# Up projection: the order of the products with the high and the low weights inside a part of the weight stream

## The chip, the core and the metric

The kernel runs on one core of one Trainium2 chip. The metric is the time of one execution on the device in microseconds (us), taken as the median over several runs. All times of engines come from one profiled execution of the program.

## What is computed

One decoder layer over 256 tokens of width 2048: a mixer (a recurrent group and an attention group side by side), then a gated feed-forward block, then a norm. The part that matters here is the feed-forward block, whose first matrix product is the up projection:

```python
xn = rms_norm(h, g_ffn[l])
u_ff, v_ff = jnp.split(xn @ w_up[l], 2, axis=-1)
u_ff = causal_dwconv(u_ff, ffn_conv_w[l], ffn_conv_b[l])
h = h + (jax.nn.gelu(u_ff) * v_ff) @ w_down[l]
return rms_norm(h, g_final)
```

Here `w_up` is 2048 x 12288 and `w_down` is 6144 x 2048, in float32.

## The kernel before, in words

**Two parts of every number.** Both factors of a product are float32. Each is cut into a high and a low part, so that the cheap float32r products lose little: high x high + high x low + low x high. The activations are kept as tiles `act` of [128 channels, 4 contraction tiles, 2 parts, 256 tokens]. The weights are split when they arrive: ACT writes the high part (`hi`, line 282) and DVE the low part (`lo`, line 283).

**The weight stream.** All weights pass through one list, `parts`. `group` (line 249) makes the parts of a block of columns. For the up projection a group is 256 columns by 16 contraction tiles; it is loaded in two DMAs of 1 MB on the SP queue (line 272, buffer `raw`, 3 of them) and worked through in four parts of 4 contraction tiles each. `run_stream` (line 287) walks the list: it issues loads 5 parts ahead, splits 2 parts ahead, and then calls the product function of the part once for each of its contraction tiles. There are 4 buffers for `hi` and 4 for `lo`; a split writes a buffer only once the products of the part four places earlier have released it. After the last part of a group its `post` function takes the sums out of PSUM.

**The up projection.** `mm_weights_still` (line 325) keeps the weights stationary: 128 x 128 weights are loaded into TensorE, and the activations stream past. For one contraction tile and one of the two halves m of the 256 columns it issues two products into PSUM bank m. The *high product* (line 336) has the high weights stationary and streams both parts of the activations, 512 columns, into the whole bank. The *low product* (line 339) has the low weights stationary and streams the high part of the activations, 256 columns, into the bank's second half. So one contraction tile gives high, low, high, low, and each product brings a weight load of its own (PEld in the profile). In the last contraction tile of a group the order is low, high, low, high, since the high product closes the bank. `halves` adds the two halves of each bank at the end, `post_up_u` and `post_up_v` do the convolution, the activation and the gating.

**Around it.** The feed-forward width is worked through in three pieces. A piece is 16 groups of the up projection (64 parts, 1024 products), then 4 groups of the down projection. The down projection (`moving`, lines 365 to 367) has the activations stationary and streams weights, always 512 columns. The input projection (`mm_weights_still_plain`, lines 320 to 322) has the weights stationary and streams always 256 columns. Nothing but the program's order and the waits for `hi`, `lo` and PSUM sets when a product runs. The framework may place instructions of an engine differently from the order in which they were written.

Of the kernel before, what the change touches and what calls it, by code (L numbers as in the profile page):

```python
# [15 lines left out]
P = 128  # L16
S = 256            # tokens
NB = S // P        # token blocks
D = 2048
KT = D // P        # contraction tiles of the model width  # L20
# [5 lines left out]
NC = 15            # compressed blocks  # L26
CB = 32            # tokens of a compressed block
CS = 16            # its stride
# [4 lines left out]
LOAD = 2048        # elements per partition of one weight load  # L33
PART = 1024        # elements per partition that are split and multiplied at once
LOOK_LOAD = 5      # parts by which loads run ahead
LOOK_SPLIT = 2     # parts by which the splitting runs ahead
FF_CUT = 3         # the feed-forward width is worked through in so many pieces
PACE = 655         # pace of the side work: units per contraction tile of 256 columns that it is put between
TAIL = 8           # contraction tiles at the end that finish the first token block before the second
# [5 lines left out]
class Part:  # L45
    """A piece of the weight stream: its load, and what is done with it once it is on chip."""

    def __init__(self, load, k0, nk, cols, mm, post):
        self.load, self.k0, self.nk, self.cols = load, k0, nk, cols
        self.mm, self.post, self.pre = mm, post, None  # L50
        self.hi = self.lo = None


class Lane:
    """A queue of side tasks (generators that yield the distance to their next step, in units of PACE)."""
# [22 lines left out]
def hymba_block(ctx, tc, x, g_mix, w_in, lru_conv_w, lru_conv_b, lru_wa, lru_ba, lru_wx, lru_bx, lru_lambda,  # L78
# [23 lines left out]
    # ---------------------------------------------------------------- constants and per-channel vectors  # L102
    ident = cst.tile([P, P], F32, name="ident")
    make_identity(nc, ident)
    xr = resp.tile([P, NB, D], F32, name="xr")           # the residual stream, tokens on partitions
# [8 lines left out]
    # keeps the tensor engine warm until the first operands are there  # L114
# [33 lines left out]
    # a compressed block counts for token t once it has ended: 16 n + 31 <= t  # L148
# [23 lines left out]
    # ---------------------------------------------------------------- helpers  # L172
    def inv_sqrt(v, y):
        """y = 1/sqrt(v) for [P, w]: the reciprocal's root, and a Newton step."""
        w = v.shape[-1]
        r = sm.tile([P, w], F32, name="rms_r")
        t = sm.tile([P, w], F32, name="rms_t")
        nc.vector.reciprocal(r, v)
        tc.keep_in_program_order(act(r, r, AF.Sqrt))
        if w == 1:  # L180
            stt(t, r, v, r, op0=OP.mult, op1=OP.mult)
        else:
            tt(t, r, r, op=OP.mult)
            tt(t, t, v, op=OP.mult)
        ts(t, t, -0.5, 1.5, op0=OP.mult, op1=OP.add)
        tt(y, r, t, op=OP.mult)

    def inv_rms(total, n, name):
        """1/sqrt(total/n + eps) for [P, w] sums of squares."""
# [6 lines left out]
    def across(rs, name):  # L196
        """[P, NB] per-token values to [P, S], the same on every partition."""
# [10 lines left out]
    # A float32's 24 bits in two parts of 12, which the float32r products carry without loss: [channel, tile, part, token]  # L208
# [6 lines left out]
    def two_parts(dst, src, gain=None):  # L215
        """dst [P, part, ..] = the two parts of src * gain"""
# [8 lines left out]
    def transpose_in(cg, g, dst):  # L225
        """Columns cg*512.. of the residual stream, times the gain, to [channel, token] in two parts."""
# [10 lines left out]
    junk = cst.tile([P, 512], mybir.dt.bfloat16, name="junk")   # only the sums are used  # L237

    def squares(dst, cg):
        """Sums of squares per token of columns cg*512.. of the residual stream."""  # L240
# [4 lines left out]
    # ---------------------------------------------------------------- the weight stream  # L245
# [3 lines left out]
    def group(w, c0, ncols, kts, mm_fn, post, cuts=None, row0=0):  # L249
        """Weight rows of `kts` contraction tiles by ncols columns; mm_fn(part, j, k, state, kts) per tile. One load  # L250
        is of LOAD elements, or of as many contraction tiles as `cuts` says."""
# [4 lines left out]
        for i, n in enumerate(cuts):  # L256
# [3 lines left out]
            for j in range(0, n, part_k):  # L260
                m = min(part_k, n - j)
                mine.append(Part(ld, k + j, m, ncols, (mm_fn, state, kts), post if k + j + m == kts else None))
        parts.extend(mine)
# [47 lines left out]
    def mm_weights_still_plain(src):  # L311
        """Weights stationary: [column, token], two tiles of 128 columns."""
# [12 lines left out]
    def mm_weights_still(src):  # L325
        """Weights stationary: [column, token], two tiles of 128 columns. A bank takes the products with the high
        parts in its first half, the rest in its second."""
        def fn(p, j, k, st, kts):
            if k == 0:
                st["ps"] = ps_mm.tile([P, 2, 512], F32, name="mm")  # L330
            a = src(k)
            last = k == kts - 1
            for m in range(2):
                o = st["ps"][:, m]
                wh, wl = p.hi[:, j, m * P:(m + 1) * P], p.lo[:, j, m * P:(m + 1) * P]
                both = lambda: mm(o, lhsT=wh, rhs=a.rearrange("p a s -> p (a s)"), start=k == 0, stop=last)  # L336
                if not last:
                    both()
                mm(o[:, S:], lhsT=wl, rhs=a[:, 0], start=False, stop=False)  # L339
                if last:  # L340
                    both()
        return fn

    def halves(dst, ps):
        """dst = the sum of the two halves of a bank"""
# [4 lines left out]
    def normed(a, rs):  # L350
        """a [P, pair, token] *= the tokens' 1/rms"""
        nc.gpsimd.tensor_tensor(a, a, over_pair(shared[rs]), op=OP.mult)  # L352

    def mm_weights_move(src):
        """Weights moving: [token, column], two blocks of 128 tokens."""
# [13 lines left out]
    # ---------------------------------------------------------------- the normalised input  # L369
# [34 lines left out]
    # ---------------------------------------------------------------- input projection and compressor  # L404
    kcat = mix.tile([P, KVH, 2, S], F32, name="kcat")      # keys [d, kv, branch, token]
    vnat = [mix.tile([P, NB, 2, 256], F32R, name=f"vnat{i}") for i in range(2)]   # values [token, block, branch, (kv d)]
# [14 lines left out]
    def blocks(which):  # L421
        """The overlapping blocks: token 16 n + l of block n, plus its position, in two parts."""
# [12 lines left out]
    def mm_cmp(which):  # L435
        """Stationary: both parts of the tokens l and l + 1 of every block; moving: the weights of l and l + 1. The
        products of unlike l go to rows and columns that nothing reads."""
# [52 lines left out]
    def post_values(br):  # L490
        def post(st):
# [5 lines left out]
            if br == 1:  # L497
                # sigmoid(z) = (1 + tanh(z / 2)) / 2
# [14 lines left out]
    # ---------------------------------------------------------------- attention  # L513
    # With 4 blocks of 64 tokens and 16 selected ones, the selection holds every block: its attention is the causal
    # one over all the tokens, whatever the scores of the blocks. With 256 tokens and a window of 512, so is the
    # window's, over its own keys and values.
# [4 lines left out]
    def open_mixers():  # L521
        late["at"] = mixctx.enter_context(tc.tile_pool(name="at", bufs=1))
        late["lr"] = mixctx.enter_context(tc.tile_pool(name="lr", bufs=1))
        # softplus(-lambda) = max(-lambda, 0) + log1p(exp(-|lambda|)), log1p(y) = 2 atanh(y / (2 + y))
# [22 lines left out]
    def attention(g, b):  # L547
# [3 lines left out]
        nk = b + 1                       # key blocks up to the diagonal one  # L551
# [4 lines left out]
        # compressed branch  # L556
# [13 lines left out]
        # selected and window branches  # L570
        w = nk * P
        hpb = 2 // nk                    # heads of a bank
# [22 lines left out]
        # probabilities with keys on partitions, then the products with the values of the three branches  # L595
# [42 lines left out]
    def channel_rms(sq, name):  # L638
        """1/rms per token from squares [channel of 128, token] that are summed over the tiles of channels."""
# [7 lines left out]
    # ---------------------------------------------------------------- RG-LRU  # L647
    lru_sq = cst.tile([P, S], F32, name="lru_sq")
    halfway = []                         # two of [channel, tile, (1 - a | gated input), token], for 4 tiles each
# [10 lines left out]
    def lru(i, xp):  # L660
# [24 lines left out]
        for m in range(2):  # L685
# [7 lines left out]
            # sigmoid(z) = (1 + tanh(z / 2)) / 2  # L693
            act(r[:, m], gp[:, :S], AF.Tanh, scale=0.5, bias=late["vh"][:, t:t + 1])
            act(iu[:, m], gp[:, S:], AF.Tanh, scale=0.5, bias=late["vh"][:, 8 + t:9 + t])
            # a = exp(-z); 1 - a = (1 + a) tanh(z / 2), without the cancellation
# [16 lines left out]
    def recurrence():  # L713
        room = scratch_new()
        ms = [room[:, :, h] for h in range(2)]
        for m, w in zip(ms, halfway):
            stt(m, w[:, :, 0], 2.0, w[:, :, 0], op0=OP.subtract, op1=OP.mult)                          # a^2 - 1
            nc.gpsimd.tensor_scalar(w[:, :, 0], w[:, :, 0], -1.0, 1.0, op0=OP.mult, op1=OP.add)        # a
# [30 lines left out]
    # ---------------------------------------------------------------- output projection  # L749
# [25 lines left out]
    # ---------------------------------------------------------------- feed-forward  # L775
    FT = FF // P // FF_CUT               # tiles of one piece
# [50 lines left out]
    def mm_tail(p, j, k, st, kts):  # L827
        """As mm_weights_move for the last columns, but the first token block comes to its end first."""
# [36 lines left out]
    # ---------------------------------------------------------------- the order of the stream  # L865
    wi, wo, wu, wd = w_in[0], w_out[0], w_up[0], w_down[0]
    def by_turns(a, b):
        """The parts of two groups, of which each is one load: by turns, two loads to a buffer."""
# [7 lines left out]
    # two groups at once as the columns of x come in, the first of them in smaller pieces  # L876
# [66 lines left out]
```

## Time and profile before

| | us |
|---|---|
| median of 3 runs | 1186.98 |
| lowest and highest run | 1184.58, 1187.15 |
| span of the profiled execution | 1185.0 |
| TensorE busy in it | 1169.7 |
| VectorE busy | 766.8 |
| ScalarE busy | 593.1 |

The span runs from the first to the last instruction of the program. The profile gives no separate total for that execution; its span is 1.98 us below the median of the runs. A start in the timeline is the moment at which the engine begins an instruction. Since TensorE overlaps the end of one product with the beginning of the next, the durations of neighbouring products overlap, and the cost of a product is the step from its start to the next start. The chain of waits shows the same as pieces that don't overlap.

### The profile page before, as it was taken

How to read it: one execution, taken by the hardware profiler on the slowest of the kernel's cores; microseconds unless marked ns; L12 is line 12 of the kernel's file. 1: busy time of each engine (PE TensorE's matmuls, PEld its weight loads, DVE VectorE, ACT ScalarE, POOL GpSimd, SP SyncE). 2: the span in 40 equal slices, each digit the busy share in tenths (PEclk: the TensorE clock that was granted, in tenths of full speed). 3: DMA queues.
4: the chain of work that ended last, by engine and by line, in shares of the span. 5: the costliest groups of instructions: out<-in, count | busy, mean ns of one | idle time of the engine just before them, and what ended most of it. 6: DMA issues, size and time to landing. Idle time of an engine off the chain costs nothing.

```text
span 1185.0 us, 16730 instructions
## 1 busy us (share of the span) xinstructions
PE 1169.7 (99%) x6727; PEld 1021.5 (86%) x6727; DVE 766.8 (65%) x981; ACT 593.1 (50%) x803; POOL 159.5 (13%) x181
## 2 busy tenths in 40 slices
PE   8999999999999999999999999999999999999997
PEld 8999999898788888888888888888888888888885
DVE  4775778779766766666454766666454666666554
ACT  5554546786446554444333444444333454445444
POOL 3210224113200110110000110110000110110000
PEclk8999999999999999999999999999999999999999
DMA  9676544354655555565556555565555565565562
GB/s 295 178 221 213 160 134 157 121 165 136 217 192 177 176 180 192 176 200 179 204 186 196 179 194 180 178 208 182 187 204 185 176 207 180 178 193 183 194 202 81
DMA packets 182397, 217.60 MB, mean 184 GB/s; under 512 B 4064, under 2 KB 147584, under 8 KB 182192
## 3 DMA queue, kind: packets, MB, share of 16 engines
q1 hardware_dynamic: 180928, 213.07, 55.2%
q0 software_dynamic: 1072, 2.41, 0.6%
q8 instruction: 52, 0.85, 0.3%
q10 hardware_dynamic: 320, 1.06, 0.2%
q14 instruction: 25, 0.20, 0.0%
HBM read 214.43 MB, written 2.10 MB: 183 GB/s over the span
## 4 chain that ended last, share of the span: by engine, by line
PE 91%; DVE 2%; ACT 0%; issue 0%; POOL 0%; DVEq 0%
PE mm L336 30%; PE mm L339 15%; PE mm L366 9%; PE mm L367 9%; PE mm L365 9%; PE mm L322 4%; PE mm L320 4%; PE mm L321 4%; PE s L578 1%; DVE lo L283 1%; PE s L366 1%; PE s L365 1%; PE s L367 1%; PE pt L613 1%; DVE act L223 0%; PE s L604 0%
## 5 line engine op out<-in xcount | busy, mean ns | idle before, releaser
L283 DVE TENSOR_TENSOR lo<-raw,hi 128x1024 fp32r<-128x1024 f32 (+1 forms) x403 | 516.7, 1284 | 294.7 <-ACT hi L282 294.4
L282 ACT ACTIVATE hi<-raw 128x1024 fp32r<-128x1024 f32 (+1 forms) x403 | 424.3, 1055 | 427.7 <-PE mm L367 183.8
L336 PE MATMUL mm<-act,hi 128*128 128x512 f32 x1536 | 539.0, 398 | 0.0
L339 PE MATMUL mm<-act,lo 128*128 128x256 f32 x1536 | 424.2, 281 | 0.0
L336 PEld LDWEIGHTS mm<-act,hi 128*128 128x128 f32 x1536 | 285.7, 188 | 66.6
L339 PEld LDWEIGHTS mm<-act,lo 128*128 128x128 f32 x1536 | 290.6, 189 | 4.5
L366 PE MATMUL mm<-lo,act 128*128 128x512 f32 (+2 forms) x544 | 206.2, 379 | 2.1 <-DVE lo L283 2.1
L367 PE MATMUL mm<-hi,act 128*128 128x512 f32 (+2 forms) x544 | 205.9, 379 | 0.0
L365 PE MATMUL mm<-hi,act 128*128 128x512 f32 (+2 forms) x544 | 205.8, 379 | 0.0
L320 PE MATMUL mm<-act,hi 128*128 128x256 f32 x512 | 147.3, 291 | 1.8 <-ACT act L222 0.9
L322 PE MATMUL mm<-act,lo 128*128 128x256 f32 x512 | 147.9, 290 | 0.6 <-DVE lo L283 0.5
L321 PE MATMUL mm<-act,hi 128*128 128x256 f32 x512 | 147.0, 288 | 0.4 <-DVE act L223 0.4
L366 PEld LDWEIGHTS mm<-lo,act 128*128 128x128 f32 x544 | 102.3, 188 | 22.5 <-DVE lo L283 3.8
L365 PEld LDWEIGHTS mm<-hi,act 128*128 128x128 f32 x544 | 102.3, 188 | 18.9 <-issue 0.4
L367 PEld LDWEIGHTS mm<-hi,act 128*128 128x128 f32 x544 | 102.3, 188 | 18.6
L352 POOL TENSOR_TENSOR up<-up,rsb 128x512 f32<-128x512 f32 x24 | 28.6, 1190 | 593.7 <-DVE up L348 508.4
L320 PEld LDWEIGHTS mm<-act,hi 128*128 128x128 f32 x512 | 98.2, 193 | 4.9 <-issue 2.1
L322 PEld LDWEIGHTS mm<-act,lo 128*128 128x128 f32 x512 | 98.8, 193 | 3.1 <-issue 1.8
L321 PEld LDWEIGHTS mm<-act,hi 128*128 128x128 f32 x512 | 98.9, 194 | 2.2 <-issue 1.2
L347 ACT COPY ev<-mm 128x512 f32<-128x512 f32 x48 | 28.2, 587 | 87.9 <-PE mm L336 87.8
L352 POOL TENSOR_TENSOR cv<-cv,rsb 128x512 f32<-128x512 f32 x24 | 38.7, 1611 | 21.7 <-ACT cv L793 21.7
L348 DVE TENSOR_TENSOR v<-mm,ev 128x512 f32<-128x512 f32 x24 | 16.6, 692 | 29.5 <-ACT ev L347 29.5
(238 smaller groups left out, 740.0 us busy)
## 6 DMA issues: line engine op xcount, KB each, us to landing
raw<-in_w_up_dram SPq DMA_DIRECT2D x96, 1024.0 KB, 5.2
raw<-in_w_down_dram SPq DMA_DIRECT2D x48, 1024.0 KB, 5.1
raw<-in_w_in_dram SPq DMA_DIRECT2D x26, 1024.0 KB, 5.3
raw<-in_w_out_dram SPq DMA_DIRECT2D x16, 1024.0 KB, 5.1
raw<-in_w_in_dram SPq DMA_DIRECT2D x15, 512.0 KB, 5.1
xr<-in_x_dram SPq DMA_DIRECT2D x4, 512.0 KB, 7.5
raw<-in_cmp_w_k_dram SPq DMA_DIRECT2D x4, 512.0 KB, 5.5
raw<-in_cmp_w_v_dram SPq DMA_DIRECT2D x4, 512.0 KB, 5.3
```

The costliest lines, as they stand in the source:

```text
L282: act(hi[:, :n], src, AF.Copy)
L283: tt(lo[:, :n], src, hi[:, :n].bitcast(F32), op=OP.subtract)
L320: mm(o, lhsT=wh, rhs=a[:, 0], start=k == 0, stop=False)
L321: mm(o, lhsT=wh, rhs=a[:, 1], start=False, stop=False)
L322: mm(o, lhsT=wl, rhs=a[:, 0], start=False, stop=k == kts - 1)
L336: both = lambda: mm(o, lhsT=wh, rhs=a.rearrange("p a s -> p (a s)"), start=k == 0, stop=last)
L339: mm(o[:, S:], lhsT=wl, rhs=a[:, 0], start=False, stop=False)
L347: nc.scalar.copy(t, ps[:, :, S:])
L352: nc.gpsimd.tensor_tensor(a, a, over_pair(shared[rs]), op=OP.mult)
L365: keep(mm(o, lhsT=h, rhs=p.hi[:, j], start=k == 0, stop=False))
L366: mm(o, lhsT=h, rhs=p.lo[:, j], start=False, stop=False)
L367: mm(o, lhsT=l, rhs=p.hi[:, j], start=False, stop=k == kts - 1)
```

## The change

Each part gets a mark `lo_first`. In a group of four parts it is false, true, false, true. The product function still issues four products for each call, but takes them from a list over the whole part: in a part without the mark the 8 high products in a row, then the 8 low ones; in a part with the mark the 8 low ones, then the 8 high ones. So from one part to the next the kind stays the same. The number of products, their operands and their banks are as before. Lines that only lose a comment are left out.

```diff
 class Part:
...
         self.hi = self.lo = None
+        self.lo_first = False
...
     def group(w, c0, ncols, kts, mm_fn, post, cuts=None, row0=0):
...
                 mine.append(Part(ld, k + j, m, ncols, (mm_fn, state, kts), post if k + j + m == kts else None))
+        for i, p in enumerate(mine):
+            p.lo_first = i > 0 and (len(mine) - 1 - i) % 2 == 0
         parts.extend(mine)
         return mine
...
     def mm_weights_still(src):
...
         def fn(p, j, k, st, kts):
             if k == 0:
                 st["ps"] = ps_mm.tile([P, 2, 512], F32, name="mm")
-            a = src(k)
-            last = k == kts - 1
-            for m in range(2):
-                o = st["ps"][:, m]
-                wh, wl = p.hi[:, j, m * P:(m + 1) * P], p.lo[:, j, m * P:(m + 1) * P]
-                both = lambda: mm(o, lhsT=wh, rhs=a.rearrange("p a s -> p (a s)"), start=k == 0, stop=last)
-                if not last:
-                    both()
-                mm(o[:, S:], lhsT=wl, rhs=a[:, 0], start=False, stop=False)
-                if last:
-                    both()
+            tiles = [(i, m) for i in range(p.nk) for m in range(2)]
+            order = [(low,) + t for low in ((True, False) if p.lo_first else (False, True)) for t in tiles]
+            n = len(order) // p.nk
+            for low, i, m in order[j * n:(j + 1) * n]:
+                o, kk = st["ps"][:, m], p.k0 + i
+                a = src(kk)
+                w = (p.lo if low else p.hi)[:, i, m * P:(m + 1) * P]
+                if low:
+                    mm(o[:, S:], lhsT=w, rhs=a[:, 0], start=False, stop=False)
+                else:
+                    mm(o, lhsT=w, rhs=a.rearrange("p a s -> p (a s)"), start=kk == 0, stop=kk == kts - 1)
         return fn
```

## Rows read from the trace of the kernel before

**Rows 1.** The page: span, TensorE's share, the granted clock, the chain's shares.

```profile
span 1185.0 us, 16730 instructions
PE 1169.7 (99%) x6727; PEld 1021.5 (86%) x6727; DVE 766.8 (65%) x981; ACT 593.1 (50%) x803; POOL 159.5 (13%) x181
PEclk8999999999999999999999999999999999999999
PE mm L336 30%; PE mm L339 15%; PE mm L366 9%; PE mm L367 9%; PE mm L365 9%; PE mm L322 4%; PE mm L320 4%; PE mm L321 4%; PE s L578 1%; DVE lo L283 1%; PE s L366 1%; PE s L365 1%; PE s L367 1%; PE pt L613 1%; DVE act L223 0%; PE s L604 0%
```

**Rows 2.** Stretches of the three up and three down projections: busy time, clock, DMA.

```profile
core 0: us, PE busy (x) PEld busy (x) DVE busy (x) ACT busy (x) POOL busy (x), PEclk, DMA share, GB/s
371.70:553.60 181.90, 181.90 (x1038) 158.30 (x1037) 123.06 (x156) 90.47 (x112) 23.52 (x24) 1.00 0.56 183
553.60:640.60 87.00, 87.00 (x385) 72.10 (x384) 44.51 (x38) 35.04 (x34) 0.00 (x0) 1.00 0.58 194
640.60:821.40 180.80, 180.80 (x1025) 156.90 (x1024) 120.27 (x142) 86.27 (x102) 23.10 (x24) 1.00 0.57 186
821.40:908.50 87.10, 87.10 (x386) 72.10 (x385) 44.51 (x38) 35.04 (x34) 0.00 (x0) 1.00 0.57 194
908.50:1089.30 180.80, 180.80 (x1026) 157.10 (x1025) 120.23 (x142) 86.31 (x102) 22.86 (x22) 1.00 0.58 186
```

**Rows 3.** Groups by shape in the second up projection, 640.6 to 821.4 us.

```profile
L336 PE MATMUL mm<-act,hi 128*128 128x512 f32 x512 | 179.7, 399 | 0.0
L339 PE MATMUL mm<-act,lo 128*128 128x256 f32 x512 | 141.4, 281 | 0.0
L339 PEld LDWEIGHTS mm<-act,lo 128*128 128x128 f32 x512 | 96.9, 189 | 1.5
```

**Rows 4.** Chain in order of time, around the end of a group: start, length, what.

```profile
661.51 0.12 PE mm L339
661.63 0.23 PE mm L336
661.87 0.11 PE mm L339
661.98 0.23 PE mm L336
662.21 0.12 PE mm L339
662.33 0.24 PE mm L336
662.57 0.24 PE mm L339 x2
...
663.17 0.45 PE mm L336 x2
```

**Rows 5.** Timeline of TensorE in the input projection: the first row, and 43 products later.

```profile
103.75 0.28 PE L320 MATMUL mm<-act,hi 128*128 128x256 f32 x1
...
108.91 0.28 PE L321 MATMUL mm<-act,hi 128*128 128x256 f32 x1
```

**Rows 6.** Timeline of TensorE in the down projection: the first row, and 27 products later.

```profile
597.80 0.39 PE L365 MATMUL mm<-hi,act 128*128 128x512 f32 x1
...
603.92 0.39 PE L365 MATMUL mm<-hi,act 128*128 128x512 f32 x1
```

**Rows 7.** Timeline of TensorE where one group ends and the next begins.

```profile
663.00 0.62 PE L336 MATMUL mm<-act,hi 128*128 128x512 f32 x2
663.46 0.28 PE L339 MATMUL mm<-act,lo 128*128 128x256 f32 x1
```

**Rows 8.** Waits in the second up projection: us in total, times, longest.

```profile
ACT hi L282 <- PE mm L336: 52.9, 33, 1.8
DVE lo L283 <- ACT hi L282: 40.4, 33, 1.6
ACT ev L347 <- PE mm L336: 28.3, 15, 1.9
...
SPq L272 <- DVE lo L283: 113.1, 24, 6.1
```

**Rows 9.** Timeline: the splits for a group's first part, and that part's beginning.

```profile
700.03 1.06 ACT L282 ACTIVATE hi<-raw 128x1024 fp32r<-128x1024 f32 x1 [1.10 <-PE mm L336]
...
702.29 1.21 DVE L283 TENSOR_TENSOR lo<-raw,hi 128x1024 fp32r<-128x1024 f32 x1
...
708.20 0.62 PE L336 MATMUL mm<-act,hi 128*128 128x512 f32 x2
708.66 0.28 PE L339 MATMUL mm<-act,lo 128*128 128x256 f32 x1
```

## The prediction, made before the change was run

> **What bounds the kernel now.** I read the page first. TensorE is busy 99% of the span, its two lines of the up projection (336 and 339) hold 45% of the chain that ended last, and the granted clock is at its full level, 2.4 GHz, after the first of 40 slices [rows 1]. Then I cut the span into stretches: in each of the three up projections TensorE is busy for the whole stretch (180.80 of 180.80 us in the second), at clock 1.00, while VectorE is busy 120.27 us, ScalarE 86.27 us and the DMA engines 57% of the time [rows 2]. The groups of that stretch show no idle time before either product [rows 3]. So the stage is bound by TensorE's own stream, and every nanosecond that a product takes less moves the end, as long as the stream stays fed.
>
> How long does a product take? The durations of 399 and 281 ns [rows 3] overlap and can't be added. The step is the stretch over the count: 180.80 us for 512 high and 512 low products is 353.1 ns for a high and a low one together. The chain shows where it goes: high pieces of 0.23 to 0.24 us, low ones of 0.11 to 0.12 us, and three pairs, from 661.51 to 662.57, take 1.06 us [rows 4].
>
> Do products that stand among their like take as long? Two stages have such runs, each product with its own weight load. In the input projection 43 steps of 256 columns take 108.91 - 103.75 = 5.16 us, 120.0 ns each [rows 5]. In the down projection 27 steps of 512 columns take 603.92 - 597.80 = 6.12 us, 226.7 ns each [rows 6]. The two differ by 106.7 ns for 256 columns, 0.417 ns a column, which is one cycle at 2.4 GHz; so each of these products has 13.3 ns beside its columns. Together they take 346.7 ns, 6.4 ns less than the alternating pair, which has 33.1 ns beside its 768 columns (320 ns). The rows show that difference; they do not show its cause.
>
> **The change, part by part.** It removes and adds no instruction: 1536 high and 1536 low products stay, with their operands, banks, columns and weight loads. Only their order inside a part moves.
>
> *The steps.* A part is 8 high and 8 low products. The four parts of a group run high, low | low, high | high, low | low, high, and the next group begins with high. Of a group's 64 steps 30 are then from high to high (the one to the next group counted), 30 from low to low, 2 from high to low and 2 back. I leave the mixed ones at their present price. A group now: 180.80 / 16 = 11.300 us. After: 30 x 0.3467 + 2 x 0.3531 = 11.107 us. That saves 0.193 us per group, and 48 groups save 9.3 us. The handful of steps that are alike already, one of each kind per group, is inside the 11.300 us.
>
> *The bounds of this price.* No run of eight of these products exists in the trace, but runs of two do: where a group ends, two low products take 0.24 us, 120 ns each, and two high ones 0.45 us, 225 ns each [rows 4]; by their starts the two high ones take 663.46 - 663.00 = 0.46 us, 230 ns each [rows 7]. I take 226.7 because it comes from the longest run of products of 512 columns and lies between the two. At 225 the saving is 11.7 us, at 230 it is 4.5 us.
>
> *High weights first, in two parts of four.* Their low products come 8 x 226.7 ns = 1.8 us after the part's beginning, where one came 0.24 us after it. That only gives the low split more time. The high buffer is released 1.0 us earlier (1.8 in place of 2.8 us), the low one at the end of the part as now.
>
> *Low weights first, in the other two.* The low weights are wanted 0.24 us earlier than now, the high ones 8 x 120 ns = 1.0 us later. The cover is long: the high split that starts at 700.03 follows the release of a buffer by TensorE, and belongs to the part that starts with the second of the two products at 708.20; the low split that ends at 703.50 is for the same part, whose first low product starts at 708.66 [rows 9]. 5.2 us of lead less 0.24 us stays 4.9 us. I cost this at nothing. Without the cover, each of the 96 parts could wait for up to one split of 1.2 us, some 115 us; the lead would have to shrink fourfold first.
>
> *Faster use of splits and loads.* The part's period falls from 2.82 to 2.78 us. ScalarE's splits wait for TensorE's buffers (52.9 us in the stretch) and SP's loads for the splits (113.1 us) [rows 8]; no wait for a load stands there. Both have room for 2% more pace. The down projections already run at 12 x 226.7 ns = 2.72 us per part without idle time [rows 2, 6]. Cost nothing.
>
> *The group's end.* A group still closes with its high products, the last of them for contraction tile 15, so ScalarE copies the sums as soon after the end as now [rows 8]. The first part is high first, so the product that opens the bank still comes before any low one. Cost nothing.
>
> *Sum.* 9.3 us less. The profiled execution goes from a span of 1185.0 to 1175.7; the median of the runs lies 1.98 us above that span, and 1186.98 - 9.3 gives **1177.7 us**.
>
> **The rivals.** *Order makes no difference.* Each product might cost its columns and a share of its own, whatever stands beside it; the 353.1 ns would then belong to these operands (activations streaming, weights from two tiles), and the forecast would compare unlike stages. Then a group stays at 11.300 us and the kernel at 1187.0. For it: the two stages of the runs stream other data. Against: low products in pairs show 120 ns and high ones 225 to 230 here too, while a high one between two low ones takes up to 240 [rows 4, 7]. The same time would come if the framework put the products back in pairs; against that, the trace shows the written order even at the group's end. 12%, the second case included.
>
> The Trainium skill, "TensorE: Matmul & The Clock Gate", sections "Back-to-back issue gap" and "LDWEIGHTS (loading the stationary operand)", speaks for this rival: a warm product costs its columns over 2.4 GHz plus 2.5 ns, and a load of 128 columns 107 ns, which either product would cover. As an estimate from that page a group would take 32 x (215.8 + 109.2) ns = 10.40 us in either order, and the change would bring 0. The trace disagrees on the size: it shows 11.30 us for that group [rows 2].
>
> *A smaller gain.* The high step is 230 ns, as by the starts in rows 7: 1182.5. 10%.
>
> *Slower: low runs dearer, high runs no cheaper.* The low step rises from its present 117 ns (0.12, 0.12 and 0.11 [rows 4]) to 120 [rows 5], since consecutive loads, 189 ns each [rows 3], no longer find a long stream every second time. If the high step keeps its 236 ns (353.1 - 117), a group takes 30 x 0.356 + 0.706 = 11.386 us, 0.086 more; 48 groups make it 1191.1. The point that decides is a high step of 353.1 - 120 = 233.1 ns: above it the change loses. Against it are the runs of 226.7 and the pairs of 225 to 230. 7%.
>
> *Far larger.* If the runs had the columns alone, 320 ns a pair, the saving would be 1440 x 33.1 ns = 47.7 us, 1139.3. No run of like products in the trace comes near. 1%.
>
> **How the numbers follow.** The forecast has 70%, the smaller gain 10%, no difference 12%, slower 7%, far larger 1%. The range takes in the forecast with its cheaper bound (1175.3) and the smaller gain (1182.5), with 2 us on either side for the spread of the runs, which reached from 1184.58 to 1187.15: 1173.3 to 1184.5. It leaves out 20%. A difference within 0.2%, 2.4 us, can't be told from none here. Faster 81%, same 12%, slower 7%.
>
> **What the profile after would show.** Each up projection about 177.7 us long, still without idle time; starts 0.227 us apart in runs of 8 and 16 high products, 0.120 us apart in low ones; the down projections unchanged at 87 us. I am wrong if the high steps stay above 0.233 us, if the timeline still alternates, or if a low product at the head of a part waits for VectorE.

## The result: 1178.56 us, and where the time went

The changed kernel takes 1178.56 us (median of 5 runs, 1177.97 to 1178.95) against 1186.98 us before: a ratio of 0.9933 with a 95% interval of 0.9922 to 0.9944. The forecast was 1177.7.

The profiled execution has a span of 1176.6 us, 8.4 us less. The page of the changed kernel begins as follows; its last line here is the chain's shares by line, where 345 is now the high product and 343 the low one.

```profile
span 1176.6 us, 16684 instructions
...
PE 1160.9 (99%) x6727; PEld 1021.8 (87%) x6727; DVE 778.6 (66%) x981; ACT 589.7 (50%) x803; POOL 159.8 (14%) x181
...
PE mm L345 30%; PE mm L343 16%; PE mm L370 9%; PE mm L371 9%; PE mm L369 9%; PE mm L325 4%; PE mm L323 4%; PE mm L324 4%; PE s L582 1%; DVE lo L286 1%; PE s L371 1%; PE s L369 1%; PE s L370 1%; PE pt L617 1%; DVE act L224 0%; PE s L608 0%
```

TensorE still has 99% and the same number of products. The stretches of the changed kernel, cut like [rows 2], show which stage got shorter:

```profile
core 0: us, PE busy (x) PEld busy (x) DVE busy (x) ACT busy (x) POOL busy (x), PEclk, DMA share, GB/s
371.10:550.60 179.50, 179.50 (x1038) 158.66 (x1037) 126.43 (x156) 89.47 (x112) 23.64 (x24) 1.00 0.56 185
550.60:637.60 87.00, 87.00 (x385) 72.06 (x384) 44.49 (x38) 35.01 (x34) 0.00 (x0) 1.00 0.58 195
637.60:815.80 178.20, 178.20 (x1026) 157.48 (x1025) 124.54 (x142) 85.20 (x102) 23.22 (x24) 1.00 0.58 189
815.80:902.80 87.00, 87.00 (x385) 72.04 (x384) 44.49 (x38) 35.01 (x34) 0.00 (x0) 1.00 0.57 195
902.80:1080.90 178.10, 178.10 (x1025) 157.44 (x1024) 124.55 (x142) 85.22 (x102) 22.99 (x22) 1.00 0.58 188
```

From the first start of an up projection to the first start of the down projection behind it, the second one takes 178.13 us (before 180.80), and so does the third; the first takes 179.47 (181.84). That is 2.37 + 2.67 + 2.67 = 7.7 us. The two ends of the second one, whose difference is the 178.13 us:

```profile
637.63 0.39 PE L345 MATMUL mm<-act,hi 128*128 128x512 f32 x1
...
815.76 0.39 PE L369 MATMUL mm<-hi,act 128*128 128x512 f32 x1
```

The first up projection also begins 0.6 us earlier, and the down projections keep their 87 us. 7.7 + 0.6 is nearly all of the 8.4 us. But the 0.6 us do not come from the change: the products ahead of the up projection are the same in both kernels and in the same order, and an early one (`pt<-ident,xr`) already starts at 24.54 us, not at 25.18. So these two executions put the change at 7.7 us.

The chain of waits of the changed kernel (start, length, what) shows the new order and the step in it, where [rows 4] had single pieces:

```profile
637.79 1.81 PE mm L345 x8
639.60 1.91 PE mm L343 x16
641.52 3.65 PE mm L345 x16
645.17 0.47 PE mm L343 x4
```

Eight high products take 1.81 us, 226 ns each; sixteen low ones 1.91 us, 119 ns each; the sixteen high ones behind them 3.65 us, 228 ns each. The groups by shape and the waits of the second up projection, against [rows 3, 8], show that nothing new holds TensorE up: there is no idle time before either product, ScalarE still waits for TensorE's buffers, and SP still waits for VectorE's splits.

```profile
L345 PE MATMUL mm<-act,hi 128*128 128x512 f32 x512 | 122.3, 391 | 0.0
L343 PE MATMUL mm<-act,lo 128*128 128x256 f32 x512 | 66.4, 283 | 0.0
...
ACT hi L285 <- PE mm L345: 48.0, 33, 2.7
...
SPq L275 <- DVE lo L286: 112.2, 24, 5.9
```

### The profile page after: what moved, and what is told of

It is laid out like the page before. It is cut to its first block, busy times and chain, and to the rows that moved or that the text cites. A ratio compares the mean times of both kernels' runs of the same rounds, so it can differ in the third digit from the quotient of the medians.

```text
span 1176.6 us, 16684 instructions
## 1 busy us (share of the span) xinstructions
PE 1160.9 (99%) x6727; PEld 1021.8 (87%) x6727; DVE 778.6 (66%) x981; ACT 589.7 (50%) x803; POOL 159.8 (14%) x181
## 4 chain that ended last, share of the span: by engine, by line
PE 91%; DVE 2%; ACT 0%; issue 0%; POOL 0%; DVEq 0%
PE mm L345 30%; PE mm L343 16%; PE mm L370 9%; PE mm L371 9%; PE mm L369 9%; PE mm L325 4%; PE mm L323 4%; PE mm L324 4%; PE s L582 1%; DVE lo L286 1%; PE s L371 1%; PE s L369 1%; PE s L370 1%; PE pt L617 1%; DVE act L224 0%; PE s L608 0%
## 5 line engine op out<-in xcount | busy, mean ns | idle before, releaser
L286 DVE TENSOR_TENSOR lo<-raw,hi 128x1024 fp32r<-128x1024 f32 (+1 forms) x403 | 527.6, 1316 | 248.2 <-ACT hi L285 248.1
L345 PE MATMUL mm<-act,hi 128*128 128x512 f32 x1536 | 367.7, 391 | 0.0
L343 PEld LDWEIGHTS mm<-act,lo 128*128 128x128 f32 x1536 | 197.3, 191 | 7.7
L343 PE MATMUL mm<-act,lo 128*128 128x256 f32 x1536 | 199.8, 283 | 0.0
L325 PE MATMUL mm<-act,lo 128*128 128x256 f32 x512 | 147.8, 289 | 0.1
L325 PEld LDWEIGHTS mm<-act,lo 128*128 128x128 f32 x512 | 98.7, 193 | 2.8 <-issue 1.8
L352 DVE TENSOR_TENSOR up<-mm,ev 128x512 f32<-128x512 f32 x24 | 16.6, 692 | 49.5 <-ACT ev L351 49.5
```

Of the source, the lines that this page charges most:

```text
L286: tt(lo[:, :n], src, hi[:, :n].bitcast(F32), op=OP.subtract)
L325: mm(o, lhsT=wl, rhs=a[:, 0], start=False, stop=k == kts - 1)
L343: mm(o[:, S:], lhsT=w, rhs=a[:, 0], start=False, stop=False)
L345: mm(o, lhsT=w, rhs=a.rearrange("p a s -> p (a s)"), start=kk == 0, stop=kk == kts - 1)
```

## The experiments

The first up projection begins between 369.5 and 372.2 us in these builds (run 11 apart), though the products ahead of it are the same in the same order. Part of that is the clock: over the first 100 us the granted clock averages 0.98 of full speed in run 12, which begins at 369.5, and 0.95 in run 5, which begins at 372.2. This moves a kernel's time by up to 2.7 us for reasons that have nothing to do with the order inside a part. Besides, the builds of this section were timed once each, runs 3 and 11 apart. So the verdicts go by the length of the second up projection, from its first start to the first start behind it; the third one repeated it within 0.01 us in every run. Each is compared with 180.80 before and 178.13 after.

I call a change from high to low and back one *change*. A group had 31 of them before and has 2 now. At the steps of long runs, 32 x 346.7 ns, a group would take 11.094 us. It took 11.300 before, 0.206 too much or 6.6 ns for each change, and takes 178.13 / 16 = 11.133 now, 0.039 too much or 19.5 ns for each.

**1. Runs of two.** The order within each contraction tile is high, high, low, low.

```diff
+            run = 1
+            if j % run:
+                return
+            tiles = [(i, m) for i in range(j, j + run) for m in range(2)]
+            last = p.k0 + j + run == kts
+            todo = [(low,) + t for low in ((True, False) if last else (False, True)) for t in tiles]
```

> Runs of two: high, high, low, low for each contraction tile (15 changes from high to low and back per group, 31 in the kernel before, 2 in the changed one). A group at the steps of long runs, 32 x 346.7 ns, is 11.094 us; before it had 0.206 us on top (6.6 ns for each change there and back), after it has 0.039 us (19.5 ns each). Theory 'a price per change': 19.5 ns each, a group of 11.386 us, an up projection of 16 groups in 182.2 us, longer than before (180.80). Rival 'each change costs 6.6 ns': 11.193 us, 179.1 us. Rival 'the price is paid by the first products behind a change, as the changed kernel's trace has them' (first two high ones 15.8 ns too long, first two low ones 7.5 ns too short): 11.218 us, 179.5 us.

Measured: 178.65 us (the kernel 1178.51). Runs of two bring four fifths of the gain: 11.166 us a group, 4.8 ns for each of 15 changes. That is below what any of the three theories allowed; a price of 19.5 ns for every change is ruled out. The chain shows the pairs:

```profile
701.55 0.23 PE mm L343 x2
701.78 0.47 PE mm L345 x2
```

Two low products take 0.23 us and two high ones 0.46 or 0.47, where long runs would give 0.24 and 0.45: the low ones are shorter here and the high ones longer.

**2. Runs of four.** The same with `run = 2`, where every second call issues nothing.

> Runs of four: two contraction tiles high, then low (7 changes there and back per group). Theory 'a price per change', 19.5 ns each: a group of 11.231 us, an up projection of 179.7 us. Rival 'each change costs 6.6 ns': 11.140 us, 178.2 us. Rival 'paid by the first products' (first four high ones 22.5 ns too long, low ones 7.5 ns too short, 15 ns per change): 11.199 us, 179.2 us.

Measured: 179.41 us (the kernel 1181.94). 11.213 us a group, 17 ns for each of 7 changes: worse than runs of two, near the third theory's 179.2 and the first one's 179.7. The price of a change thus depends on the runs around it: 6.6 ns in strict alternation, 4.8 in runs of two, 17 in runs of four, 19.5 in long ones. There is no single price, and fewer changes are not always better. Four high ones take 0.93 us here, against 0.91 at the step of long runs, and four low ones 0.47, against 0.48:

```profile
651.40 0.93 PE mm L345 x4
652.33 0.47 PE mm L343 x4
```

**3. One change in a group.** High products of the first two parts, low ones of all four, high ones of the last two.

```diff
+            part = p.k0 // p.nk
+            new = lambda q, low: [(q, low, i, m) for i in range(q.nk) for m in range(2)]
+            held = st.setdefault("held", [])
+            if j == 0:
+                held.append(p)
...
+            if part == 0:
+                todo = new(p, False)[2 * j:2 * j + 2]
+            elif part == 1:
+                todo = (new(p, False) + new(held[0], True) + new(p, True))[6 * j:6 * j + 6]
+            elif part == 2:
+                todo = new(p, True)[2 * j:2 * j + 2]
+            else:
+                todo = (new(p, True) + new(held[2], False) + new(p, False))[6 * j:6 * j + 6]
```

> Runs of 32: high products of the first two parts, low ones of all four, high ones of the last two, so one change there and back per group where the changed kernel has two. Price per change of 19.5 ns: a group of 11.114 us, an up projection of 177.8 us (changed kernel 178.13), 0.9 us less in all than the changed kernel, some 1177.6 us. Rival: holding two parts at once releases buffers later, low splits come late and TensorE waits: idle time at low products' line, an up projection above 178.2 us.

Measured: 177.81 us, as expected by the price between long runs, and 1177.31 us for the kernel (5 runs, 1177.15 to 1178.02; ratio to the kernel before 0.9925, interval 0.9912 to 0.9939). Its chain shows runs of 16 and 32:

```profile
637.23 3.63 PE mm L353 x16
640.86 3.83 PE mm L351 x32
```

The three stretches are 0.3 us shorter each than those of the changed kernel. So this version is ahead of both, by about 1 us of the changed kernel; the intervals of the two ratios overlap, and it is the stretches that tell them apart.

**4. Other banks.** The old alternation, but a low product never follows a high one into the same PSUM bank. A group's first and last contraction tile have runs of two, so that there are 29 changes in place of 31.

```diff
+            H, L = False, True
+            if k == 0:
+                todo = [(H, j, 0), (H, j, 1), (L, j, 0), (L, j, 1)]
+            elif k == kts - 1:
+                todo = [(L, j, 0), (L, j, 1), (H, j, 0), (H, j, 1)]
+            else:
+                m = 1 - k % 2
+                todo = [(H, j, m), (L, j, 1 - m), (H, j, 1 - m), (L, j, m)]
```

> The old alternation of high and low products, but consecutive products never go to the same PSUM bank (high in one, low in the other). If the extra time of the alternation comes from a low product that follows a high one into the same bank, the pair falls from 353.1 ns to about 346.7 ns and an up projection to about 177.7 us. If it comes from the change between 512 and 256 columns, nothing changes: 180.8 us.

Measured: 180.79 us. Six alternating pairs between the two starts below take 2.12 us, 353 ns each as before. The banks have no part in it.

```profile
699.85 0.23 PE mm L347
...
701.97 0.23 PE mm L347
```

**5 and 6. Equal widths.** The low product streams both parts of the activations, so it has 512 columns too; once in the old alternation, once in the changed order.

```diff
...
-                    mm(o[:, S:], lhsT=w, rhs=a[:, 0], start=False, stop=False)
+                    mm(o, lhsT=w, rhs=a.rearrange("p a s -> p (a s)"), start=False, stop=False)
```

> The old alternation, but the low product streams both parts of the activations, 512 columns, as the high one does (the small product low x low comes in addition). Loads, weight tiles and banks alternate as before; only the widths are equal. Theory 'the change of width costs': no extra, 453.4 ns a pair (2 x 226.7), an up projection of 232.1 us, the kernel some 154 us longer than before. Rival 'the change of weight tile or of bank costs': the pair keeps its 6.4 ns, 459.8 ns, 235.4 us.

> The changed order (runs of 8 and 16), with the low product on 512 columns as well. Theory 'the change of width costs': the same as the alternating one with equal widths, 232.1 us for an up projection. Rival 'the change of weight tile or of bank costs': 232.1 us here, but 3.3 us less than the alternating one.

Measured: 232.106 us alternating and 232.107 in runs, against 232.1 expected. The stretch of each, alternating first, then in runs:

```profile
692.70:924.80 232.10, 232.10 (x1025) 192.26 (x1024) 121.42 (x142) 86.92 (x102) 23.19 (x24) 1.00 0.45 148
```

```profile
691.90:924.00 232.10, 232.10 (x1026) 192.19 (x1024) 123.41 (x142) 85.26 (x102) 20.74 (x24) 1.00 0.45 147
```

With equal widths the order makes no difference at all. Weight tiles, loads and banks alternated as before, so the extra time of the alternation needs neighbours of unequal width. With 512 columns everywhere no load stands beside a short stream either; but that alone isn't the cause, as the input projection, 256 columns everywhere, steps evenly at 120.0 ns [rows 5].

**7. Short high loads.** The old alternation, with 64 stationary columns for the high product.

```diff
...
-                    mm(o, lhsT=w, rhs=a.rearrange("p a s -> p (a s)"), start=kk == 0, stop=kk == kts - 1)
+                    c = P if kk in (0, kts - 1) else 64
+                    mm(o[:c], lhsT=w[:, :c], rhs=a.rearrange("p a s -> p (a s)"), start=kk == 0, stop=kk == kts - 1)
```

> The old alternation, but the high product keeps only 64 of its 128 stationary columns, except in a group's first and last contraction tile (the upper half of its sums is left out), so the weight load that stands beside the short low stream is half as long. Rival 'the load of the high weights doesn't fit beside 256 columns': the pair falls from 353.1 to 346.7 ns or less, an up projection to 177.7 us or less. Theory 'the change of width costs': 180.8 us, as before.

Measured: 176.26 us, below every run with full loads. So the number of stationary columns does enter, and the theory that only the streams' widths count falls. The edit shortens the weight load and also narrows the high product itself; no run separates the two. The timeline of this kernel (start, length) shows how they lie:

```profile
644.04 0.39 PE L342 MATMUL mm<-act,hi 128*64 128x512 f32 x1
644.04 0.19 PEld L339 LDWEIGHTS mm<-act,lo 128*128 128x128 f32 x1
...
644.26 0.28 PE L339 MATMUL mm<-act,lo 128*128 128x256 f32 x1
644.27 0.13 PEld L342 LDWEIGHTS mm<-act,hi 128*64 128x64 f32 x1
644.38 0.39 PE L342 MATMUL mm<-act,hi 128*64 128x512 f32 x1
...
644.72 0.39 PE L342 MATMUL mm<-act,hi 128*64 128x512 f32 x1
```

A load starts just when the product before its own starts. Halving its columns shortens its row from 0.19 to 0.13 us. The pair takes 0.34 us, from 644.04 to 644.38 to 644.72, and the chain shows that the high product is at the step of long runs, 0.227 us, and the low one below its own, at 0.11 in place of 0.120 us, though the edit left it alone.

```profile
644.20 0.23 PE mm L342
644.42 0.11 PE mm L339
```

This is so in every second group only. By their first starts the groups take 10.93 and 11.11 us by turns, and in the longer ones three pairs take 1.04 us, 347 ns each:

```profile
655.11 0.39 PE L342 MATMUL mm<-act,hi 128*64 128x512 f32 x1
...
656.15 0.39 PE L342 MATMUL mm<-act,hi 128*64 128x512 f32 x1
```

The program is the same in both, so one sequence of products can fall into either of two steps, and it keeps the one it has to the group's end. Nothing here shows what chooses.

**8. Short low loads.** The old alternation, with 64 stationary columns for the low product.

```diff
...
-                    mm(o[:, S:], lhsT=w, rhs=a[:, 0], start=False, stop=False)
+                    mm(o[:64, S:], lhsT=w[:, :64], rhs=a[:, 0], start=False, stop=False)
```

> The old alternation, but the low product keeps only 64 of its 128 stationary columns (the upper half of its sums is left out). Its weight load stands beside the 512 columns of the high product before it. Theory 'only a load that stands beside 256 columns costs': nothing changes, 353.1 ns a pair, an up projection of 180.8 us. Rival 'any shorter load or narrower product saves': the pair falls by some 10 ns as it did with short high loads, an up projection of about 176.3 us.

Measured: 177.80 us, 347.3 ns a pair. Neither theory holds: halving the load beside the long stream saves too, 3.0 us in the stretch where run 7 saved 4.5.

**9. Short low loads in the changed order.** The same edit on the changed kernel.

> The changed order, but the low product keeps only 64 of its 128 stationary columns (the upper half of its sums is left out). In a run of low products their loads stand beside 256 columns. Theory 'a load that stands beside 256 columns costs': the low step falls from 120 ns to about 113 ns, as the low step has it with short high loads in the alternation; a group is about 32 x 340 ns + 0.04 = 10.92 us, an up projection 174.7 us. Rival 'the width of the neighbour costs, not the load': 120 ns, 178.1 us.

Measured: 175.15 us, close to the 174.7 of the load theory. The chain of this kernel has the run of low products that took 1.91 us with full loads:

```profile
641.91 1.82 PE mm L340 x16
643.73 1.39 PE mm L342 x6
```

1.82 us for 16 is 114 ns each. So in a run of low products it is the number of stationary columns that holds the step at 120 ns. That it is their load, and not the width of the product, is argued from run 7, where a low product of full width came to 0.11 us as well. The six high ones behind them still take 1.39 us, 232 ns each.

**10. Short high loads in the changed order.** The edit of run 7 on the changed kernel.

> The changed order, but the high product keeps only 64 of its 128 stationary columns, except in a group's first and last contraction tile (the upper half of its sums is left out). In a run of high products their loads stand beside 512 columns; only the first of a run loads beside a low one. Theory 'a load that stands beside 256 columns costs': high steps stay at 226.7 ns and low ones at 120, and the five high steps behind a change, now 27 ns too long in sum, come down to at most 10 ns; an up projection between 177.5 and 177.9 us (changed kernel 178.13). Rival 'shorter high loads save wherever they stand', 10 ns a pair: about 173 us.

Measured: 178.67 us, longer than with full loads (178.13) and outside both expectations. The chain shows it in the high products:

```profile
640.99 1.91 PE mm L340 x16
642.90 3.67 PE mm L343 x16
```

The low ones keep 119 ns; sixteen high ones take 3.67 us, 229 ns each, where 3.65 us was the value with full loads. Their starts never settle at 226.7 ns: they lie between 224 and 236 ns apart to the end of the run. A shorter load in a long run of high products is no gain, and in part a loss. I have no account of that.

**11. The input projection too.** On top of run 3, the input projection's three products of 256 columns per contraction tile and half became one of 512 and one of 256, with a function that adds the halves before each `post`.

```diff
+    def summed(post):
+        def fn(st):
+            ps = st["ps"]
+            t = ev.tile([P, 2, S], F32, name="ev")
+            nc.scalar.copy(t, ps[:, :, S:])
+            tt(ps[:, :, :S], ps[:, :, :S], t, op=OP.add)
+            post(st)
+        return fn
```

> As the run with one change per group, and the input projection's products of 256 columns in the same way: per contraction tile and half one high product of 512 and one low of 256 columns in place of three of 256, in runs. By the steps 346.7 ns replace 3 x 120.0 = 360 ns, 13.3 ns times 512 = 6.8 us less, some 1170.5 us, if the sum of the two halves that each of 16 groups needs in addition (a copy of 0.59 us on ScalarE, an addition of 0.69 us on VectorE) is hidden. Rival: VectorE and ScalarE are busier in that stretch and hand on the groups later, TensorE waits for splits or attention, and the gain is lost: 1177 us or more.

Measured: 1186.48 us (11 runs; ratio to the kernel before 1.0004, interval 0.9995 to 1.0014). The rival held, and more: the whole gain of run 3 is gone. The stretches ahead of the up projection, first of this kernel, then of run 3:

```profile
0.00:100.00 100.00, 89.98 (x513) 77.51 (x514) 63.27 (x107) 55.35 (x83) 21.31 (x38) 0.93 0.74 223
200.00:280.00 80.00, 77.55 (x449) 65.43 (x448) 64.08 (x108) 59.04 (x104) 16.93 (x25) 1.00 0.47 149
280.00:380.00 100.00, 96.00 (x422) 78.00 (x421) 73.81 (x100) 54.56 (x82) 21.67 (x19) 0.97 0.55 185
```

```profile
0.00:100.00 100.00, 94.96 (x718) 90.85 (x719) 63.51 (x107) 55.69 (x82) 24.33 (x38) 0.97 0.78 230
200.00:280.00 80.00, 80.00 (x607) 74.49 (x606) 62.07 (x102) 59.56 (x100) 18.25 (x26) 1.00 0.47 152
280.00:370.00 90.00, 87.97 (x397) 71.34 (x396) 66.60 (x83) 47.03 (x66) 15.60 (x15) 1.00 0.55 188
```

TensorE idles 10.0 us in the first 100 us in place of 5.0, 2.4 us between 200 and 280 in place of none, and 4.0 us in the last stretch in place of 2.0; its granted clock averages 0.93 in place of 0.97 at the start and 0.97 in place of 1.00 in the last stretch. The up projection begins at 380.2 us, not at 370.9, and then runs at the 177.81 us of run 3. The 9.3 us are as much as the added idle time, 5.0 + 2.4 + 2.0 us. The lower clock is a loss of its own: by the means, 7 and 3 us of full speed are missing in the two stretches, where run 3 misses 3, and the 7 us more, an estimate, are as much as the merged products should have saved. The timeline shows one place where the two meet:

```profile
308.72 0.77 PE L394 MATMUL mm<-hi,act 128*128 128x512 f32 x1 [3.14 <-DVE xr L799]
...
310.13 0.63 PE L394 MATMUL mm<-hi,act 128*128 128x512 f32 x1
310.56 0.63 PE L395 MATMUL mm<-lo,act 128*128 128x512 f32 x1
```

TensorE has waited 3.14 us for VectorE, and the products of 512 columns behind the wait start 0.43 us apart, not 0.227; the granted clock is 0.50 from 308.7 to 314.4 us, the lower of its two levels (1.2 GHz), and 1.00 again from 315. The other waits were not taken apart.

**12. Without half of the marks.** Only a group's last part has its low products first.

```diff
-            p.lo_first = i > 0 and (len(mine) - 1 - i) % 2 == 0
+            p.lo_first = i > 0 and i == len(mine) - 1
```

> One part of the change undone: only the last part of a group has its low products first, the other three their high ones, so there are 3 changes there and back per group in place of 2, with runs of 8 (high in front of low) and one of 16 low ones. At the 19.5 ns that a change costs between long runs (39 ns for 2 in the changed kernel, 19 ns for 1 in the run with one change per group) a group takes 11.094 + 0.0585 = 11.153 us and an up projection 178.4 us, 0.9 us more in all than the changed kernel. Rival, by the runs of four (17 ns) and two (4.9 ns): shorter runs pay less per change, up to 178.2 us.

Measured: 178.45 us, as expected from 19.5 ns for each of 3 changes. The chain shows the runs of eight:

```profile
650.38 1.84 PE mm L345 x8
652.22 0.95 PE mm L343 x8
653.17 1.84 PE mm L345 x8
```

Eight high products behind low ones take 1.84 us, 26 ns more than 8 x 226.7, and the eight low ones 0.95, up to 10 ns less than 8 x 120. So the alternating marks of the change are worth 0.3 us in each up projection; the runs of eight are worth the rest.

## Why the prediction was right

**The bound.** Right. The stage was TensorE's own stream, and it stayed so: no idle time, and the down projections unchanged.

**The steps of runs.** Right. High products in runs take 226 to 227 ns, low ones 119 to 120, as the other two stages had them [rows 5, 6]. The pair of two high ones at the end of a group, between 225 and 230 [rows 4, 7], had bounded it from both sides.

**The mixed steps.** Here a term was mis-sized. I left them at the present price, 353.1 ns for a pair, so that each change cost 6.4 ns over the run's 346.7. Between long runs a change costs 19.5 ns: the first five high products behind low ones are 27 ns too long together, the first two low ones behind high ones some 8 ns too short. With 2 changes in each of 48 groups that is 1.3 us, which is most of the difference between the 9.3 us of the sum and the 7.7 us measured in the up projections. The other 0.3 us is the first projection, which gained less than the other two; some 13 products of other lines lie in it, before and after (x1038 against x1025), and why it gained less was not taken apart. It is partly luck that the forecast came within 0.9 us of the median: in the profiled executions 0.6 us of the gain lies ahead of anything that the change touches, and without it the forecast would be 1.5 us off.

**The costs of nothing.** Right where they can be read: no wait for a low split at the head of a part, none for a load, no later evacuation.

**The rivals.** That order makes no difference fell for these widths, though with equal widths it is true to 0.001 us (runs 5 and 6). The Trainium skill's rule in "TensorE: Matmul & The Clock Gate", sections "Back-to-back issue gap" and "LDWEIGHTS (loading the stationary operand)", had spoken for it: columns over 2.4 GHz plus 2.5 ns, which the first section gives as the gap of isolated products, and a load of 107 ns, an estimate from the second, that either product covers. The trace disagrees with the first part: products in runs have 13.3 ns beside their columns [rows 5, 6]. The smaller gain had high steps of 230 ns throughout; only the first ones behind a change are that long. The rival that ended slower needed high steps above 233.1 ns; runs have 227.

**What stays open.** The prediction said that the rows show the difference and not its cause. The runs narrow it down. It needs neighbours of unequal width (runs 5, 6), not shared banks (run 4), and it depends on the number of stationary columns (runs 7, 8, 9), which sets the length of the load and the width of the product together; that the load is what counts is argued, not shown. But no rule of mine forecast all of it: not the two steps of run 7, not the saving from a load that stands beside 512 columns (run 8), not the loss from short loads in a long high run (run 10), nor why runs of two are better than runs of four. A run without any weight load was not tried, as every product here brings its own.

## What to carry to other kernels

Where TensorE is the bound and each product brings its own weight load, the cost of a product is the step between starts, and products of equal width in a row can be cheaper than the same products mixed. Another stage of the same kernel that already runs in the wanted order gives that step, but the seams between runs need a price of their own, since they cost more than the mixture suggests. Merging products to save steps did not pay where TensorE also waits for other engines: in the input projection the added waits, and the lower clock that came with them, cost the whole gain of run 3.

## What the hardware showed that was not expected

A weight load starts within 0.01 us of the start of the product ahead of its own, and its row shrinks from 188 to 134 ns when 64 of 128 columns are left out (runs 7 and 9): 54 ns for 64 columns, so about 107 ns for 128 beside a fixed part. The Trainium skill, "TensorE: Matmul & The Clock Gate", section "LDWEIGHTS (loading the stationary operand)", has a load take its columns over 1.2 in ns, as an estimate 107 ns for 128; the trace's slope agrees with that. A stream of 256 columns lasts 256 x 0.417 = 106.7 ns by the slope between [rows 5] and [rows 6], so the two are as good as equal, and with half the load a low product is 6 ns shorter (run 9). That the load sets its step is not shown by this: products of 512 columns, whose stream is twice as long, have the same 13.3 ns beside their columns [rows 6].

The steady steps lie near multiples of 6.67 ns, sixteen columns at 2.4 GHz: 113.3, 120.0 and 226.7 ns are 17, 18 and 34 of them, and the alternating pairs of 340.0 (every second group of run 7), 346.7 (its other groups, and run 8 away from a group's ends) and 353.3 ns (before) are 51, 52 and 53. That is an observation over these runs; nothing here explains it.
